# A 64 KB write of zeros issued beside the first load of a rotation kernel

## The chip, the cores and the metric

The kernel runs on one core of a Trainium2 chip. The metric is the device time of one execution in microseconds (us), lower is better. The profile is one execution, whose span (first to last instruction) is some 1.8 us shorter than the time.

## The reference

```python
batch, c, h, w = 32, 3, 256, 256
x = np.random.randn(batch, c, h, w).astype(np.float32)
np.rot90(x, k=1, axes=(-2, -1)).astype(np.float32)
```

96 images of 256 x 256 floats are rotated by a quarter turn. There is no arithmetic. 25.17 MB are read and 25.17 MB are written.

## The kernel before

The 96 images go through in 6 groups of 16, 4 MB each. All transfers between the chip's main memory and its on-chip buffer are made by 16 DMA engines, in packets (here each is one contiguous piece, mostly a whole row). Loads are issued from SyncE (queue q1 in the profile) into a tile S, VectorE (DVE) rotates S into U with transposes, and stores are issued from ScalarE (ACT, queue q10). S and U have three buffers each. Groups 0 and 5 (kind 1) move in four parts with rows of 8 KB, which lets the first store start early and the last one end early. Groups 1 to 4 (kind 2) move in two halves with rows of 16 KB.

```python
KINDS = [1, 2, 2, 2, 2, 1]
...
in_pool = ctx.enter_context(tc.tile_pool(name="in_pool", bufs=3))
out_pool = ctx.enter_context(tc.tile_pool(name="out_pool", bufs=3))

for g, kind in enumerate(KINDS):
    S = in_pool.tile([P, F], fp32, name="S")
    U = out_pool.tile([P, F], fp32, name="U")
    if kind == 1:
        ...
        for s in range(4):
            nc.sync.dma_start(out=Sv[:, s], in_=xv[s])          # 1 MB, rows of 8 KB
        for s in range(4):
            src = ...; dst = ...
            nc.vector.transpose(dst, src)
            nc.scalar.dma_start(out=ov[s], in_=Uv[:, s])
    else:
        ...
        for b in range(2):
            nc.sync.dma_start(out=Sv[:, b], in_=xv[b])          # 2 MB, rows of 16 KB
        ...
        for q in range(R):
            nc.vector.transpose(dst[:, q], src[:, q])
        for a in range(2):
            nc.scalar.dma_start(out=ov[a], in_=Uv[:, a])
```

Of the kernel before, what the change touches and what calls it, by code (L numbers as in the profile page):

```python
# [1 line left out]

# [4 lines left out]


@with_exitstack
def kernel(  # L10
    ctx: ExitStack,
    tc: tile.TileContext,
    x: bass.AP,
    out: bass.AP,
):
    nc = tc.nc
    B, C, H, W = x.shape
    assert H == W == 256
    N = B * C
    P = 128  # L20
    G = 16
    KINDS = [1, 2, 2, 2, 2, 1]
    assert len(KINDS) * G == N
    F = G * H * W // P
    fp32 = mybir.dt.float32

    xf = x.rearrange("b c h w -> (b c h w)").rearrange("(g f) -> g f", g=N // G)
    of = out.rearrange("b c h w -> (b c h w)").rearrange("(g f) -> g f", g=N // G)

    in_pool = ctx.enter_context(tc.tile_pool(name="in_pool", bufs=3))  # L30
    out_pool = ctx.enter_context(tc.tile_pool(name="out_pool", bufs=3))

    for g, kind in enumerate(KINDS):
        S = in_pool.tile([P, F], fp32, name="S")
        U = out_pool.tile([P, F], fp32, name="U")
        if kind == 1:

            R = 8
            Sv = S.rearrange("p (s f) -> p s f", s=4)
            Uv = U.rearrange("p (s f) -> p s f", s=4)  # L40
            xv = xf[g].rearrange("(s p f) -> s p f", s=4, p=P)
            ov = of[g].rearrange("(s p f) -> s p f", s=4, p=P)
            for s in range(4):
                nc.sync.dma_start(out=Sv[:, s], in_=xv[s])  # L44
            for s in range(4):

                src = Sv[:, s].rearrange("p (r k q) -> p q r k", r=R, q=R)[:, ::-1, :, ::-1]
                dst = Uv[:, s].rearrange("p (q k r) -> p q r k", q=R, r=R)
# [5 lines that stand above are left out]
            R = 16  # L54
            Sv = S.rearrange("p (b f) -> p b f", b=2)
            Uv = U.rearrange("p (a f) -> p a f", a=2)
            xv = xf[g].rearrange("(b a qk f) -> b qk a f", b=2, a=2, f=F // 2)
            ov = of[g].rearrange("(b a qk f) -> a qk b f", b=2, a=2, f=F // 2)
            for b in range(2):
                nc.sync.dma_start(out=Sv[:, b], in_=xv[b])  # L60

            src = Sv.rearrange("p b (r k q) -> p q r k b", r=R, q=R)[:, ::-1, :, ::-1]
            dst = Uv.rearrange("p a (q k r) -> p q r k a", q=R, r=R)
# [6 lines that stand above are left out]
# [1 line left out]
_INS = ['x']  # L71
_OUTS = [((32, 3, 256, 256), 'float32')]


# [23 lines left out]
```

## Time and profile before

| | before |
|---|---|
| time, median of the first 4 runs (range) | 124.02 us (123.87 to 124.13) |
| span of the profile | 122.2 us |
| DVE busy | 91.3 us, 75% |
| DMA moved | 50.34 MB, mean 412 GB/s over the span |
| first load packet starts / last store packet ends | 1.75 us / 121.06 us |

The head of the page of the kernel before: busy time of each engine, then the span in 40 slices of 3.06 us (9 means 90% busy or more), and the rate in each slice.

```profile
span 122.2 us, 170 instructions
DVE 91.3 (75%) x72; POOL 0.2 (0%) x4
...
DVE  0199999007999999999999990799999999092000
...
DMA  3999999999999999999999999999999999999993
GB/s 86 424 421 416 375 432 429 426 410 442 418 440 437 437 434 418 429 434 429 429 429 429 434 429 421 453 410 413 464 413 429 445 416 426 442 429 408 429 429 161
DMA packets 4609, 50.34 MB, mean 412 GB/s; under 512 B 512, under 2 KB 512, under 8 KB 512
```

The DMA row is full in 38 of 40 slices, while DVE has gaps. The kernel is bound by its DMA engines, from the second slice to the last but one.

One slice shows less: the fifth (12.2 to 15.3 us) has 375 GB/s. The windows view shows it better with a window laid around it (columns: start and end of the window in us, its length, busy DVE and instructions, busy POOL, TensorE clock, DMA share, GB/s):

```profile
core 0: us, DVE busy (x) POOL busy (x), PEclk, DMA share, GB/s
8.50:11.50 3.00, 3.00 (x2) 0.00 (x0) 1.00 1.04 434
11.50:14.50 3.00, 3.00 (x2) 0.00 (x0) 1.00 1.02 366
15.00:18.00 3.00, 3.00 (x2) 0.00 (x0) 1.00 1.00 423
```

Between 11.5 and 14.5 us the rate falls to 366 GB/s although the engines count as busy. I call this **the dip**. The packet records under these windows say what happens (start and end in ns from the start of the span, queue, bytes, duration in ns). The prediction counted these times from a first load packet put at 1.70 us; from the start of the span they are 0.05 us later.

```
13584 14576 1 16384 992
13680 14716 1 16384 1036
13841 14150 10 8192 309
13879 14188 10 8192 309
```

The first store packets (queue 10) arrive at 13.84 us and take 309 ns each, as all 8 KB packets do in a full stream. The load packets just before them take up to 1,036 ns, where 16 KB packets usually take 611. To measure a dip I sum, from the packet records in the packed trace (no view of the profile prints them), over all data packets that begin in a window, the time above the usual time of their size (309 ns for 8 KB, 611 for 16 KB), and divide by 16 engines. I call this sum excess packet time. For 11 to 15 us this gives 0.50 us.

### The profile page before, as it was taken

To read this page: it belongs to the slowest core of one execution; us is meant where nothing else is said; L and a number is where in the kernel's file an instruction comes from. 1 tells how busy PE (TensorE), PEld (TensorE's weight loads), DVE (VectorE), ACT (ScalarE), POOL (GpSimd) and SP (SyncE) were. 2 spreads that over 40 slices of the span, in tenths; PEclk is the share of its full clock that TensorE was granted. 3 is DMA by queue.
4 is the path that set the end of the run, shared out by engine and by line. 5 is a ranking of instruction groups with operands and counts; after the bars stand their busy time and mean duration, and the time that the engine had idled before them with its cause. 6 is when DMAs were issued, how large, how long until landed. Compare 5 with 4: busy or idle time off the path is not lost.

```text
span 122.2 us, 170 instructions
## 1 busy us (share of the span) xinstructions
DVE 91.3 (75%) x72; POOL 0.2 (0%) x4
## 2 busy tenths in 40 slices
DVE  0199999007999999999999990799999999092000
POOL 0000000000000000000000000000000000000000
DMA  3999999999999999999999999999999999999993
GB/s 86 424 421 416 375 432 429 426 410 442 418 440 437 437 434 418 429 434 429 429 429 429 434 429 421 453 410 413 464 413 429 445 416 426 442 429 408 429 429 161
DMA packets 4609, 50.34 MB, mean 412 GB/s; under 512 B 512, under 2 KB 512, under 8 KB 512
## 3 DMA queue, kind: packets, MB, share of 16 engines
q1 hardware_dynamic: 2304, 25.17, 49.3%
q10 hardware_dynamic: 2304, 25.17, 48.3%
q14 instruction: 1, 0.01, 0.0%
HBM read 25.17 MB, written 25.17 MB: 412 GB/s over the span
## 4 chain that ended last, share of the span: by engine, by line
DMA 61%; DVE 27%; issue 1%; SPq 1%
DMA S<-in_x_dram 46%; DVE U L65 24%; DMA out_dram<-U 16%; DVE U L49 3%; SPq L44 1%
## 5 line engine op out<-in xcount | busy, mean ns | idle before, releaser
L65 DVE STREAM_TRANSPOSE U<-S 128x512 f32<-128x512 f32 x64 | 60.5, 1059 | 10.8 <-DMA S<-in_x_dram 7.1
L49 DVE STREAM_TRANSPOSE U<-S 128x2048 f32<-128x2048 f32 x8 | 31.0, 3937 | 8.7 <-DMA S<-in_x_dram 8.7
L82 POOL MEMSET const-bfloat16-1.0<- 128x1 bf16 x1 | 0.1, 101 | 0.0
L82 POOL MEMSET const-uint8-127<- 128x1 uint8 x1 | 0.1, 101 | 0.0
L82 POOL MEMSET const-float32-0.0<- 128x1 f32 x1 | 0.1, 98 | 0.2 <-issue 0.2
L82 POOL MEMSET const-float32-1.0<- 128x1 f32 x1 | 0.1, 98 | 0.0
## 6 DMA issues: line engine op xcount, KB each, us to landing
S<-in_x_dram SPq DMA_DIRECT2D x8, 2048.0 KB, 21.1
out_dram<-U ACTq DMA_DIRECT2D x8, 2048.0 KB, 19.0
S<-in_x_dram SPq DMA_DIRECT2D x8, 1024.0 KB, 16.6
out_dram<-U ACTq DMA_DIRECT2D x8, 1024.0 KB, 16.1
```

The lines of the kernel that those rows point to most:

```text
L44: nc.sync.dma_start(out=Sv[:, s], in_=xv[s])
L49: nc.vector.transpose(dst, src)
L65: nc.vector.transpose(dst[:, q], src[:, q])
L82: nc = _bacc.Bacc("TRN2", target_bir_lowering=False, num_devices=1)
```

## The change

The change sends 64 KB of zeros to the last-stored part of the output, from the store queue, beside the first load. The text of the change gives no reason. The likely intent is to make the first use of the write path fall into the time when the engines are still starting up, rather than at 13 us. The zeros are overwritten by the last store some 110 us later, so the result is unchanged.

```diff
     in_pool = ctx.enter_context(tc.tile_pool(name="in_pool", bufs=3))
     out_pool = ctx.enter_context(tc.tile_pool(name="out_pool", bufs=3))
+    zero = ctx.enter_context(tc.tile_pool(name="zero", bufs=1)).tile([P, 128], fp32, name="zero")
+    nc.vector.memset(zero[:], 0.0)
+    last = of[N // G - 1].rearrange("(s p f) -> s p f", s=4, p=P)[3]
+    nc.scalar.dma_start(out=last[:, :128], in_=zero[:])
```

The write takes 512 B from each of 128 partitions, one packet each, 8 packets for each DMA engine.

## The prediction

> **What bounds it now.** DMA. In the page's 40 slices the DMA row is 9 in 38; DVE is busy 75% and waits for loads. 25.17 MB come in and 25.17 MB go out. An 8 KB packet takes 309 ns, a 16 KB one 611 ns, so the data packets cost 16 engines an estimated 118 us of the 122.2 us span. The Trainium skill ("DMA: Bandwidth & Descriptors", "Where 436 GB/s comes from") puts the ceiling at 435 GB/s; the packet records' 427 to 432 agree within 2%. Left over, from the packet records:
> - 1.70 us before the first load packet;
> - about 0.5 us in which the first 128 load packets run cold (mean 374 ns, the worst 1,366 ns);
> - a dip at 11.5 to 14.5 us where the first store begins: load packets take up to 1,036 ns instead of 611, some 231 KB are missed, an estimated 0.54 us. Later store starts cost little (at 47 to 50 us an estimated 0.08 us);
> - 1.2 us from the last packet to the end.
>
> So hardly more than 1 us can be won by anything done early.
>
> **What the change does.** The likely intent is to make the first write during the engines' cold start, so that the dip at 13 us does not come. It removes no work. It adds one 128x128 memset on DVE (idle to 5.67 us, so free); one issue on ACT (0.34 us like its other stores of 8 KB rows; ACT is idle to 9.67 us, so free); and 128 packets of 512 B, 8 for each engine. By rate these cost 64 KB / 427 GB/s = 0.15 us, with a fixed part for each packet an estimated 0.2 to 0.3 us. That is on the critical path unless it falls into the cold stall at 1.7 to 3 us. I expect the first zero packet at about 2 us if it goes straight to the engines (the first load took 0.97 us from issue to first packet). The first store's packets came 4 us after its issue, behind loads already queued; like that it would come at 4 to 6 us, in the full stream. Semaphores: the static order shows the same waits shifted by one lane; no load waits for a different transfer, and the last store's ordering behind the zeros is met some 100 us earlier.
>
> **Two outcomes, about equally likely.** (a) The dip is a first-write cost and vanishes or shrinks: minus 0.2 to 0.5 us, plus about 0.2 us of packets. (b) It comes from elsewhere (the switch from 8 KB to 16 KB loads, new addresses) and stays: plus 0.15 to 0.3 us. Either is below 0.5%.
>
> Predicted 123.85 us, range 123.3 to 124.4 us. Faster by over 2%: 0.01 (no 2.5 us are there to win). Within 2%: 0.97. Slower by over 2%: 0.02.
>
> **What would show it.** Right: DMA row unchanged; 144 packets more (128 data, 16 semaphore); DVE total up by 0.1 to 0.2 us only. For (a): the slice at 12.2 to 15.3 us, 375 GB/s before, rises to about 425. For (b): it stays below 390 and everything after it moves by 0.1 to 0.3 us. Wrong: load packets at 2 to 6 us stretched by more than 0.5 us, so that the first transpose starts later than 6.3 us (5.67 before).
>
> **What would make it wrong.** The small writes stall single engines, so that the slowest one, which sets the end (the last engine finished one packet, 0.3 us, after the others), falls behind; or the early write changes the steady rate of the mixed stream, for which I see no mechanism.

## The result, and the profile after

| | before | after |
|---|---|---|
| time, median of 4 runs (range) | 124.02 us (123.87 to 124.13) | 124.19 us (124.12 to 124.26) |
| ratio, 95% interval | | 1.0015 (0.9997 to 1.0032) |
| span | 122.2 us | 122.5 us |
| last store packet ends | 121.06 us | 121.33 us |
| dip at 11 to 15 us, excess packet time | 0.50 us | 0.51 us |

Ratios here and below are the mean time of one kernel's runs over that of the other's of the same rounds, so they are not quite the ratio of the medians quoted.

The interval includes 1, so these runs alone do not show that the change costs anything. What the zeros cost is worked out below from larger writes. These are the lines of the page after that answer to those shown of before, with the lines for the new instructions:

```profile
span 122.5 us, 173 instructions
DVE 91.5 (75%) x73; POOL 0.2 (0%) x4
...
DVE  0199999006999999999999991699999999191000
...
DMA  3999999999999999999999999999999999999994
GB/s 99 420 428 407 409 399 431 449 420 417 452 399 433 460 433 342 428 428 428 428 428 450 439 439 423 425 447 399 433 439 415 452 433 407 455 433 393 428 428 185
DMA packets 4753, 50.41 MB, mean 412 GB/s; under 512 B 528, under 2 KB 656, under 8 KB 656
...
L35 DVE MEMSET zero<- 128x128 f32 x1 | 0.2, 165 | 0.8 <-PEq L88 0.8
...
out_dram<-zero ACTq DMA_DIRECT2D x1, 64.0 KB, 5.0
```

The memset costs DVE 0.165 us at 0.8 us, when DVE has nothing to do. There are 144 packets more (128 data, 16 for the semaphore). The DMA row is as full as before. The zeros land 5.0 us after their issue.

The dip is still there:

```profile
core 0: us, DVE busy (x) POOL busy (x), PEclk, DMA share, GB/s
8.50:11.50 3.00, 3.00 (x2) 0.00 (x0) 1.00 1.02 429
11.50:14.50 3.00, 3.00 (x2) 0.00 (x0) 1.00 1.07 385
```

By the packet records it is as large as before (0.51 against 0.50 us). The first zero packet starts at 4.60 us, 3.6 us after its issue began at 1.02 us, and the last ends at 5.56 us. So the zeros did not meet idle engines. Load packets ran while they waited, and they ran in the middle of the full stream. Where they waited, and why so long, no run here shows.

One more difference catches the eye: the slice of 342 GB/s at 45.9 to 49.0 us (418 before). There a second, smaller dip cost 0.40 us of packet time after and 0.08 before. Further profiles give no sign that this belongs to the change: the changed kernel again gave 0.16 us, late_store, which turned out to be the old program again, gave 0.14, and memset_only, which writes no zeros, 0.28.

### The profile page after: what moved, and what is told of

Its sections match the earlier page's. It is cut to its first block, busy times and chain, and to the rows that moved or that the text cites. A ratio compares the mean times of both kernels' runs of the same rounds, so it can differ in the third digit from the quotient of the medians. Undisturbed runs are those within 1.5% of the kernel's fastest.

```text
span 122.5 us, 173 instructions
## 1 busy us (share of the span) xinstructions
DVE 91.5 (75%) x73; POOL 0.2 (0%) x4
## 4 chain that ended last, share of the span: by engine, by line
DMA 69%; DVE 20%; SPq 0%; issue 0%
DMA S<-in_x_dram 38%; DMA out_dram<-U 31%; DVE U L55 13%; DVE U L71 8%; SPq L50 0%
```

## The experiments

Variants of the zeros are shown as edits of the changed kernel; late_store, one_store and the kinds variants are edits of the kernel before. The first question was what the zeros cost and why. The second was what the dip belongs to, since the change was to remove it.

### What the zeros cost

**after_again** is the changed kernel once more.

> The changed kernel once more (a comment apart), to see what repeats. Theory P (packets): the zeros cost only their own time on the DMA engines, 128 packets of 27 ns over 16 engines, an estimated 0.22 us, in a stream with no slack: 124.1 to 124.3 us, and the zero packets again at about 4.5 us. Rival N (noise): the 0.17 us measured was chance: within 0.05 us of before. The dips at 11.5 to 14.5 us and at 47 to 49 us: if they belong to the kernel they come again with the same size; if the 47 us one (0.39 us after, 0.08 before) differs by more than 0.2 us from the last profile, it varies from run to run and says nothing of the change.

Measured: 124.14 us (124.00 to 124.29, 5 runs), ratio 1.0006 (0.9994 to 1.0019). The zeros started at 4.91 us. The dip was 0.37 us and the one at 47 us 0.16 us. So the dips come back in the same places, but their sizes vary by 0.1 to 0.2 us between profiles.

**memset_only** keeps the memset and drops the write.

```diff
-    last = of[N // G - 1].rearrange("(s p f) -> s p f", s=4, p=P)[3]
-    nc.scalar.dma_start(out=last[:, :128], in_=zero[:])
```

> The memset stays, the write of zeros goes. Theory P: the memset is free because DVE is idle until 5.7 us: 124.0 us, within 0.05 us of before. Rival M (the cost lies with the added DVE instruction or the longer program): 124.2 us, like the changed kernel.

Measured: 123.98 us (123.97 to 124.02, 5 runs), ratio 0.9993 (0.9980 to 1.0007). The memset is free. The slowest of the five runs (124.02) lies below eight of the nine runs of the changed kernel.

**zero_8x512** and **zero_1x4096** write eight times the bytes, one in 1,024 packets of 512 B and the other in 128 packets of 4 KB.

```diff
-    zero = ... .tile([P, 128], fp32, name="zero")
+    zero = ... .tile([P, 1024], fp32, name="zero")
...
# zero_8x512: every second 512 B of the last 1 MB
-    nc.scalar.dma_start(out=last[:, :128], in_=zero[:])
+    cols = last.rearrange("p (c f) -> p c f", f=128)[:, ::2, :]
+    nc.scalar.dma_start(out=cols, in_=zero.rearrange("p (c f) -> p c f", f=128))
# zero_1x4096: the first 4 KB of each row
+    nc.scalar.dma_start(out=last[:, :1024], in_=zero[:])
```

> The zeros as 1,024 packets of 512 B (512 KB) in one transfer. Theory P: 64 packets of 27 ns for each engine, 1.73 us: 125.7 us. Rival B (only the bytes cost, at the rate of the stream, 427 GB/s): 1.23 us: 125.2 us. Rival F (a fixed cost of an early transfer, or of the shifted lanes): 124.2 us, as with 64 KB.

> The same 512 KB as 128 packets of 4 KB. Theory P: 8 packets for each engine of an estimated 156 ns (half of 309 and a few), 1.25 us: 125.25 us, 0.4 to 0.5 us faster than zero_8x512. Rival B: the same as zero_8x512. Rival F: 124.2 us.

Measured: zero_8x512 125.30 us (125.26 to 125.82, 4 runs), ratio 1.0109 (1.0090 to 1.0129). zero_1x4096 125.35 us (125.32 to 125.39, 4 runs), ratio 1.0104 (1.0090 to 1.0117). Before, in the same rounds, 124.07 us. The cost of 512 KB is 1.23 and 1.28 us by the medians. The rate of the stream gives 524,288 B / 427 GB/s = 1.23 us. Eight times as many packets for the same bytes gave the same time within 0.05 us. Theory P (27 ns for each packet, so 1.73 us for zero_8x512 and 0.4 to 0.5 us less for zero_1x4096) does not fit: by its interval zero_8x512 cost 1.12 to 1.60 us, and the gap is missing. Theory B fits: the zeros cost about their bytes. For 64 KB that is 0.15 us.

A smaller cost for each packet is not excluded by these times. The Trainium skill ("DMA: Bandwidth & Descriptors", "Why small descriptors are slow (HBM only)") gives each packet a fixed overhead of about 3 cycles. An estimate by that formula for 512 B is 16 + 3 = 19 cycles, 19% on top of the bytes, or 0.23 us for the 512 KB; 4 KB packets would pay 2% (if the trace's packets are the page's). The intervals above are about 0.2 us wide on either side, and the two kernels did not lose the same elsewhere: over the whole span the excess packet time was 1.18 us in zero_8x512 and 1.46 us in zero_1x4096, whose 4 KB zeros made a dip of their own (below).

The packet records of zero_8x512 can be asked without the dips. Between 14 and 22 us no packet is stretched. The 16 engines moved 202 loads of 16 KB and 216 zeros there in 16 x 8 us (a packet that crosses the edge counts in part). A 16 KB packet takes 608 ns of an engine where the stream has no others (kinds_222221 at 5 to 28 us: 605 of them, excess left out). That leaves an estimated 22 to 24 ns for each zero, where its share of the bytes would be 19 ns. So the 3 to 5 ns more for each packet do agree with the skill's formula (3 of 19 cycles), and come to an estimated 0.2 to 0.3 us for 1,024 packets, hidden in the total by the smaller dips. For the 128 packets of the change it is an estimated 0.03 us. The recorded 27 ns are too much to add up: with them, the packets between 14 and 22 us would fill 1.1% more time than there was.

zero_8x512 also shows how the two queues share an engine. Between 14 and 22 us, 216 zeros and 200 loads of 16 KB began, about one for one, and the zeros took until 29.7 us to drain, so that the first real store, issued at 9.72 us, began only at 28.78 us (some engines were done with the zeros earlier). This agrees with the Trainium skill (the same page, "Queues, rings and completion order"), which says that an engine takes turns between queues at the grain of a packet (one for one is as the trace counts packets; a packet of the page can hold several pieces). These are the issues of the ACT queue in zero_8x512 (start and length in us):

```profile
1.96 0.62 ACTq L38 DMA_DIRECT2D out_dram<-zero  x1
9.72 20.77 ACTq L57 DMA_DIRECT2D out_dram<-U  x4
```

That a delay of 15 us against before (13.84 us) cost hardly more than the bytes shows how little the stores' start matters here while loads fill the engines.

**zero_16x4096** writes the original 64 KB as 16 packets of 4 KB.

```diff
-    zero = ... .tile([P, 128], fp32, name="zero")
+    zero = ... .tile([16, 1024], fp32, name="zero")
...
-    nc.scalar.dma_start(out=last[:, :128], in_=zero[:])
+    nc.scalar.dma_start(out=last[:16, :1024], in_=zero[:])
```

> The same 64 KB as 16 packets of 4 KB, one for each engine. Theory B (the zeros cost their bytes at the stream's rate, 0.15 us, whatever the packet size): 124.15 us. Rival P (a cost for each packet; fewer packets are cheaper): 124.05 us or less. If a single large write for each engine were enough to take the dip away: 123.8 us and the dip at 12 to 14 us below 0.2 us.

Measured: 124.26 us (124.05 to 124.36, 4 runs), ratio 1.0021 (1.0006 to 1.0036), before in the same rounds 123.95 us. The time is not below that of the 128-packet write, so no gain from fewer packets is seen (the 0.03 us estimated above are far below what these runs resolve). The dip was 0.35 us.

**zero_before_load** issues the zeros on the loads' queue.

```diff
-    nc.scalar.dma_start(out=last[:, :128], in_=zero[:])
+    nc.sync.dma_start(out=last[:, :128], in_=zero[:])
```

> The 64 KB of zeros on the same queue as the loads and ahead of them, so that they meet idle engines. The first load is issued after the memset and the zeros' issue, some 0.3 + 0.4 us later than before, and nothing later can win that back in a stream with no slack: 124.6 to 124.8 us. If the early write warms anything that matters (the cold start of the loads, 0.3 to 0.5 us, or the dip at 11.5 to 14.5 us), the packet records show it gone and the time stays below 124.3 us.

Measured: 124.17 us (124.05 to 124.46, 4 runs), ratio 1.0006 (0.9991 to 1.0021), before 124.09 us. The experiment missed its point. The scheduler put the zeros after the first load, because they wait for the memset, so nothing was delayed by 0.7 us and the expected 124.6 us does not apply. The first zero packet came at 5.05 us, and the cold start of the loads (0.72 us of excess before 4 us, by the same sum) was already over. The dip was 0.20 us, the smallest of this shape. Whether zeros that really meet idle engines would be free stays untested.

### What the dip belongs to

**zero_first** writes the zeros where the first store will write.

```diff
-    last = of[N // G - 1].rearrange("(s p f) -> s p f", s=4, p=P)[3]
-    nc.scalar.dma_start(out=last[:, :128], in_=zero[:])
+    first = of[0].rearrange("(s p f) -> s p f", s=4, p=P)[0]
+    nc.scalar.dma_start(out=first[:, :128], in_=zero[:])
```

> The same 64 KB of zeros, into the region that is stored first (512 B of each of the 128 rows of the first store). Theory A (addresses of the output are cold at their first write): the dip at 11.5 to 14.5 us shrinks from 0.36 to 0.51 us to below 0.2 us, and the time is 123.9 us. Theory S (any start of a store stream in full rows dips, cold addresses or not): dip 0.35 to 0.5 us as in the changed kernel, time 124.15 us.

Measured: 124.10 us (124.05 to 124.28, 4 runs), ratio 1.0013 (0.9998 to 1.0028), before 123.95 us. The dip was 0.30 us: neither below 0.2 as theory A needs nor in the 0.35 to 0.5 that theory S named. The time gives no sign of a gain.

**late_store** was to hold the first stores back.

```diff
                 nc.vector.transpose(dst, src)
-                nc.scalar.dma_start(out=ov[s], in_=Uv[:, s])
+                if g > 0:
+                    nc.scalar.dma_start(out=ov[s], in_=Uv[:, s])
+            if g == 0:
+                for s in range(4):
+                    nc.scalar.dma_start(out=ov[s], in_=Uv[:, s])
```

> The kernel before, with the four stores of group 0 issued together after its fourth transpose (at 21 us instead of 9.7, 13.5, 17.3, 21.1 us). It tells apart what the dip at 11.5 to 14.5 us belongs to. Theory S (the store stream's start): loads run at 427 GB/s through 11 to 20 us and the dip of 0.3 to 0.5 us comes where the first store packets come, at 21 to 26 us. Rival L (the switch from 8 KB to 16 KB load packets, or the new load addresses): the dip stays at 12 to 14 us, where the first 16 KB loads come. The total may be up to some us longer, because loads wait for the later stores.

Measured: 123.90 us (1 run, state unknown). The edit changes nothing: stores are the only work of the ACT queue and each waits for its own transpose, so the instruction order on every engine stayed that of before. It serves as a second profile of the kernel before: dip 0.54 us, first store packet at 13.84 us. An order in the source is not an order in time.

**kinds_112221** removes the change of load size at 12 us.

```diff
-    KINDS = [1, 2, 2, 2, 2, 1]
+    KINDS = [1, 1, 2, 2, 2, 1]
```

> The kernel before with group 1 also as kind 1 (8 KB rows), so that the loads do not change size at 12 us and the store queue does not run empty at 42.6 us. Theory S: the dip at 12 to 14 us stays at 0.3 to 0.5 us, because the first store starts there as before; the one at 47 us (0.08 to 0.40 us in four profiles) goes, because the store queue is not empty before it; 8 KB packets cost 512 x (309 - 305.5) ns / 16, 0.11 us, more: 123.8 to 124.0 us. Rival L: the dip at 12 to 14 us goes, and one comes where the first 16 KB loads come.

Measured: 124.47 us (124.38 to 124.50, 4 runs), ratio 1.0039 (1.0023 to 1.0056). The dip stayed, at 0.64 us. The windows view of kinds_112221:

```profile
core 0: us, DVE busy (x) POOL busy (x), PEclk, DMA share, GB/s
11.50:14.50 3.00, 3.00 (x2) 0.00 (x0) 1.00 0.99 330
30.00:34.00 4.00, 3.55 (x2) 0.00 (x0) 1.00 1.03 438
```

There was none where the 16 KB loads now begin (32.3 us), and none at 47 us. So the load size is not its cause. The time was expected to fall slightly and rose by 0.5 us. Of the 0.44 us by which its span is longer, 0.27 lie before the end of the last store packet (121.33 us; the usual time of its packets is 0.22 us longer for an engine, 117.98 against 117.76 us, twice what was expected, which counted 512 of the 1,024 added packets), and 0.17 after it (1.33 us from there to the end, 1.16 before). Why the tail is longer stays open.

**one_store** holds the first store back with a real dependence: one transfer for the whole of group 0, which must wait for all four transposes.

```diff
                 nc.vector.transpose(dst, src)
-                nc.scalar.dma_start(out=ov[s], in_=Uv[:, s])
+                if g > 0:
+                    nc.scalar.dma_start(out=ov[s], in_=Uv[:, s])
+            if g == 0:
+                nc.scalar.dma_start(out=ov.rearrange("s p f -> p s f"), in_=Uv)
```

> The kernel before, with group 0 stored by one transfer of 512 rows of 8 KB after its fourth transpose (about 21 us) instead of four from 9.7 us on. (The earlier late_store left the order of instructions as it was, so it was only a repeat of the kernel before.) Theory S: no dip at 11 to 15 us, where the first 16 KB loads come, and one of 0.3 to 0.6 us just before the first store packets, at 21 to 26 us. Rival L (load size or load addresses): dip at 12 to 14 us as before. Time within 0.4 us of before either way, if the loads do not wait for the later store.

Measured: 124.16 us (124.10 to 124.24, 4 runs), ratio 1.0004 (0.9989 to 1.0018). First store packet at 24.81 us. The windows view of one_store:

```profile
core 0: us, DVE busy (x) POOL busy (x), PEclk, DMA share, GB/s
11.50:14.50 3.00, 3.00 (x2) 0.00 (x0) 1.00 1.08 459
23.00:26.00 3.00, 2.95 (x4) 0.00 (x0) 1.00 0.93 360
```

The dip at 11.5 to 14.5 us is gone (0.00 us by the packet sum, with the same loads at the same addresses in the same place), and one of 0.39 us stands at 23 to 28 us, around the first store packet. The dip belongs to the start of the stores and not to the place or size of the loads.

**kinds_222221** stores group 0 later still and in 16 KB rows.

```diff
-    KINDS = [1, 2, 2, 2, 2, 1]
+    KINDS = [2, 2, 2, 2, 2, 1]
```

> Group 0 also as kind 2: 16 KB packets from the start, first store only after its 16 transposes, at about 29 us. Theory S: no dip before 28 us, one of 0.3 to 0.6 us at 28 to 34 us. Packets: 256 of 16 KB in place of 512 of 8 KB, 0.11 us less. Time 123.7 to 124.0 us if the loads never wait; some us longer if they do (12 MB of loads are in flight until about 30 us, and the next one needs the first transposes done).

Measured: 124.81 us (124.54 to 125.09, 6 runs), ratio 1.0055 (1.0041 to 1.0069). First store packet at 33.04 us. The windows view of kinds_222221:

```profile
core 0: us, DVE busy (x) POOL busy (x), PEclk, DMA share, GB/s
11.50:14.50 3.00, 0.74 (x1) 0.00 (x0) 1.00 0.98 421
30.00:34.00 4.00, 4.00 (x5) 0.00 (x0) 1.00 1.00 340
```

Again no dip at 12 us, and one of 0.82 us just before the first store, larger than expected. The cold start is longer too (0.81 us against 0.50), the first load packet comes 0.38 us later (2.13 us), and the tail is 0.16 us longer (1.32 us). This version, which I had hoped might win, loses.

The two runs with eight times the zeros finish the picture. First the windows of zero_8x512, whose 512 B writes ran from 6.4 to 29.7 us, then those of zero_1x4096, whose 4 KB writes ran from 5.75 to 10.4 us:

```profile
core 0: us, DVE busy (x) POOL busy (x), PEclk, DMA share, GB/s
11.50:14.50 3.00, 3.00 (x2) 0.00 (x0) 1.00 1.07 445
23.00:26.00 3.00, 2.16 (x3) 0.00 (x0) 1.00 1.02 430
25.50:29.50 4.00, 4.00 (x6) 0.00 (x0) 1.00 0.96 332
```

```profile
core 0: us, DVE busy (x) POOL busy (x), PEclk, DMA share, GB/s
5.00:7.00 2.00, 1.22 (x1) 0.00 (x0) 1.00 1.01 350
11.50:14.50 3.00, 3.00 (x2) 0.00 (x0) 1.00 0.98 380
```

In zero_8x512, 22 us of small writes to the output did not spare the full-row stores their dip. It came at 26 to 30 us (0.57 us), just before the first 8 KB store packet at 28.78 us, and not at 12 us. That store had been issued at 9.72 us, about when the kernel before issues its own (9.67 us), so the dip goes with the first packets of the store and not with its issue. In zero_1x4096 the zeros themselves made a dip when they started (0.43 us at 4 to 7.5 us), and the stores at 13.4 us still made another (0.27 us).

| kernel | zeros | first full-row store packet, us | dip, excess packet time, us | ratio |
|---|---|---|---|---|
| before / late_store | none | 13.84 / 13.84 | 0.50 / 0.54 at 11 to 15 | 1 / not timed in rounds |
| memset_only | none | 13.76 | 0.37 at 11 to 15 | 0.9993 |
| after / after_again | 64 KB | 13.92 / 13.51 | 0.51 / 0.37 at 11 to 15 | 1.0015 / 1.0006 |
| zero_first | 64 KB, first region | 13.42 | 0.30 at 11 to 15 | 1.0013 |
| zero_16x4096 | 64 KB, 16 packets | 13.37 | 0.35 at 11 to 15 | 1.0021 |
| zero_before_load | 64 KB, load queue | 13.36 | 0.20 at 11 to 15 | 1.0006 |
| zero_8x512 | 512 KB, 512 B | 28.78 | none at 11 to 15; 0.57 at 26 to 30 | 1.0109 |
| zero_1x4096 | 512 KB, 4 KB | 13.44 | 0.43 at 4 to 7.5; 0.27 at 11 to 15 | 1.0104 |
| one_store | none | 24.81 | none at 11 to 15; 0.39 at 23 to 28 | 1.0004 |
| kinds_222221 | none | 33.04 | none at 11 to 15; 0.82 at 31 to 35 | 1.0055 |
| kinds_112221 | none | 13.39 | 0.64 at 11 to 15 | 1.0039 |

What is shown: in every profile a dip stands just before or around the first store in full rows, wherever that is, and it moves when that store moves. What is not settled: why the loads stall there, and whether an early write makes it a little smaller. With 64 KB of zeros the dip was 0.20 to 0.51 us in five profiles (mean 0.35); without, at the same place and shape, 0.37 to 0.54 in three (mean 0.47). The ranges overlap. None of the versions with zeros was faster than before. A restart of the stores after a pause dips at 47 us in the kernel before, but in kinds_112221 (66.7 us) and zero_1x4096 (50.3 us) it did not, so a pause alone does not explain a dip either.

One_store also shows that a saving in the mean need not reach the end. Its engines were busy with data 118.62 us on average against 118.99 before, yet its last packet ended only 0.09 us earlier (120.97 us) and its time was the same. A likely reason, not tested, is that the last engine sets the end and not the mean one. The time after the last packet was 0.19 us longer (1.35 against 1.16 us). So removing the dip may be worth less than its 0.5 us.

## Why the prediction was right or wrong

The time was right: 123.85 us predicted, 124.19 measured, inside the range of 123.3 to 124.4. The point estimate was 0.34 us low. Being inside the range says little: the range covers both outcomes of the prediction, and the kernel before (124.02 us) lies in it too. What follows looks at the steps (the prediction's points are given in short).

- **"What bounds it now: DMA."** Right. 512 KB of zeros in place of 64 KB cost 1.23 to 1.28 us over the kernel before, about what the stream needs for these bytes (1.23 us). No slack hid them.
- **"The memset is free, the ACT issue is free."** Right for the memset: 0.165 us on an idle DVE, and memset_only ran at 0.9993 of before. For the issue no run separates it, but ACT's first store still began at 9.75 us (9.67 before), right after the first transpose.
- **"0.15 us by rate, with a fixed part for each packet 0.2 to 0.3 us."** The mechanism (added bytes in a full stream) was right, but the fixed part was put too high. The prediction's 0.2 us and more comes from 8 packets of the recorded 27 ns for each engine; worked out from the stream's time, a packet of 512 B takes 22 to 24 ns, 3 to 5 ns more than its bytes. The cost is an estimated 0.18 us, nearly all of it bytes. The difference measured between after and before was 0.17 us and 0.07 us in the two comparisons, neither clear of noise by itself.
- **"First zero packet at about 2 us if it goes straight to the engines, at 4 to 6 us if behind loads."** The second: 4.60 us in one profile and 4.91 in the other.
- **"(a) The dip is a first-write cost and vanishes or shrinks."** This half of the bet failed. It is what put the estimate 0.34 us too low: 123.85 us is about what (a) alone gives (124.02 less 0.35 plus 0.2). The dip was 0.51 us after. A first write of small packets did not pay it in advance here; not even 22 us of them did (zero_8x512).
- **"(b) It comes from elsewhere (the switch from 8 KB to 16 KB loads, new addresses) and stays: plus 0.15 to 0.3 us."** The dip stayed and the sum was right, but the cause named for it was wrong. kinds_112221 kept the dip without the switch, and one_store moved it away from the same loads. It belongs to the first stores in full rows. Both outcomes of the prediction misplaced it, in different ways.
- **The test named for (a) and (b)**, the slice at 12.2 to 15.3 us, was too coarse. It reads 375 before and 409 after, between the two thresholds of 390 and 425. Slices far from any dip swing as widely in the page after (452, 399, 433 at 31 to 40 us, where no packet is stretched). The sum over the packets decides it, the slice does not.
- **"Load packets at 2 to 6 us not stretched; the first transpose no later than 6.3 us."** Right: the first transpose began at 5.75 us (5.67 before), and the excess packet time at 2 to 6 us was 0.23 us (0.13 before), below the 0.5 us named.

## What to carry to other kernels

When the DMA engines are full from end to end, a warm-up transfer is not free because its engine is idle; it costs its bytes at the stream's rate and, in small packets, a few ns more for each, and a gain has to be seen before it is believed. An early DMA issued beside large loads need not run early: here its packets began 3.6 us after the issue, while loads ran, so look at when its packets start and not at when it is issued. Before trying to remove a dip, move the things around it one at a time (here the first store, the load size) to see what it follows. And two kernels that take the same time need not have the same costs: where dips vary by 0.3 us from kernel to kernel, look for a stretch without them before saying that a cost of 0.2 us is absent.

## What the Trainium skill lacked or had wrong

- "DMA: Bandwidth & Descriptors", "Latency and other measured facts", gives a first-byte time of about 0.6 us for transfers issued from SP or ACT, and does not say from where it counts. Here, with idle engines, the first packet came 1.02 us after the start of the issuing instruction (0.73 to 1.75 us) and 0.65 us after its end, which agrees (0.77 us in kinds_222221). Beside loads it was 3.6 to 4.2 us from the start of the issue (zeros 1.02 to 4.60 us, first store 9.67 to 13.84 us). I found no number for the second case on that page, although it describes how the queues take turns.
- No page that I read says that durations of packet records add up to more than the time: 8 KB packets are recorded with 309 ns and 512 B ones with 27 ns, but packets of 8 KB alone took 307 ns of an engine (kinds_112221 at 15 to 28 us), and those of 512 B an estimated 22 to 24 ns (zero_8x512 at 14 to 22 us).
- No page that I read has the dip: just before the first store in full rows, load packets took up to 1,036 ns instead of 611 in the kernel before, and 0.20 to 0.82 us of engine time were lost in the 13 profiles. The 64 KB writes of zeros caused no such dip when they started (about 0.02 us or less in the sum at 4 to 7.5 us); 512 KB in 4 KB rows did (0.43 us), and 512 KB in 512 B packets hardly (0.06 us).
